# Three small moves in a four-layer decoder trunk: where the first weights land, which PSUM banks two tiles use, and when a broadcast product is issued

## The chip, the cores and the metric

The kernel runs on one core of one Trainium2 chip. A core has five engines with in-order instruction queues: TensorE (PE in the rows, its weight loads PEld), VectorE (DVE), ScalarE (ACT), GpSimd (POOL) and SyncE (SP), which here issues almost all transfers. The metric is the device time of one launch in microseconds; smaller is better.

## The reference, cut to what matters

The trunk has two layers on 256 tokens of width 2048. Layer 0 mixes tokens with a gated short convolution beside a state-space scan (S5), layer 1 with window attention. Both then attend to 256 memory tokens and run a gated MLP. What the change touches is all at the start:

```python
mem_n = rms_norm(mem, norm_mem)
hn = rms_norm(h, norm_mix[0])
z = hn @ w_in                      # gate B | gate C | conv input | S5 input u
ys = s5_branch(u, ...)             # a linear recurrence over the 256 tokens
k, v = jnp.split(mem_n @ w_kv[l], 2, axis=-1)   # for both layers l
```

Everything is in float32.

## The kernel before, in words

**Products in two parts.** Every matrix is split into a rounded part `hi` and a remainder `lo`. `wload` fetches 1 MB of weights into one of three `raw` buffers (SP, line 87), casts 1024 columns at a time to `hi` on ACT (line 95), and forms `lo = raw - hi` on DVE (line 96); there are four `hi` and four `lo` buffers, which is two weight tiles. A product tile of `gemm` is 16 matmuls with `hi` (line 110, 512 columns wide: the activations' own hi and lo side by side) and 16 with `lo` (line 115). The result sits in one of four large-pool PSUM banks (`pp`, tag `ps`) until ACT copies one half out (line 206) and DVE adds the other (line 210). Four more banks (`pm`, taken by `bank()`) serve all small products.

**Order of the start.** `first_tiles` runs through the 16 blocks k of the input and of the first 512 columns of u in steps of 1, 1, 2, 2, 2, 4, 4: load x (line 294), load the weights (line 87), split x with its gain (ACT line 72, DVE line 73), square it (ACT 223, POOL 221), and multiply into four banks at once (lines 311 and 314). Then four more u tiles, n = 4 to 7, go through `gemm` (weights `win(28)` to `win(31)`); the statistics product (line 235) and the broadcast product of the input's norm stand among them. Before, all weights of this stretch rotate through the three `raw` buffers.

**The memory's keys and values.** `mem_kv(0)` then runs 16 key tiles and 4 column groups of 4 value steps (matmuls of lines 371, 372 and 376), and `mem_kv(1)` the same for layer 1. After each tile a callback pulls pieces of the S5 work (`s5`, a generator) worth about 2 us: B products (line 440, which take all four small banks and are copied out by ACT, line 442), the scan itself (ACT line 541 and DVE lines 545 to 548, each step needing the other engine's last), and the outputs (lines 564 to 577). Key tiles collect in a single buffer `kst` of four tiles; when it is full ACT's queue issues its write to DRAM (line 361) and the next tile's DVE addition waits until that has landed.

**The memory's norm.** In layer 0's keys, `mem_norm` squares the memory tokens on ACT after tiles 5 and 6, computes the reciprocal root as a column after tile 8 (`rsqrt_col`, lines 243 to 252), and after tile 10 calls `stat_bc("mem")`: two DVE instructions write a diagonal matrix into a shared temporary (line 261), two matmuls with a matrix of ones spread it to all partitions (line 263), and ACT copies the result out (line 268). Its user, the cross-attention, comes hundreds of microseconds later.

**Who orders what.** Python order is program order; a scheduling layer assigns buffers and waits and may move an instruction ahead of others that its model holds up. Each engine then executes its own list strictly in order.

Of the kernel before, what the change touches and what calls it, by code (L numbers as in the profile page):

```python
# [13 lines left out]
F32 = mybir.dt.float32  # L14
# [3 lines left out]
ALU = mybir.AluOpType  # L18
# [4 lines left out]
P = 128  # L23
T = 256
D = 2048
KT = 16
# [10 lines left out]
class Trunk:  # L37
# [42 lines left out]
        nc.vector.tensor_tensor(o[:, T:], src, o[:, :T].bitcast(F32), op=ALU.subtract)  # L80
        return o

    def wload(self, src, kt, n):

        nc = self.nc
        raw = self.rawp.tile([P, kt * n], F32, name="raw", tag="raw")
        nc.sync.dma_start(raw.rearrange("p (k n) -> p k n", n=n), src)
        kc = 1024 // n
        parts = []
        for c in range(0, kt, kc):  # L90
            m = min(kc, kt - c)
            hi = self.hip.tile([P, m * n], F32R, name="hi", tag="hi")
            lo = self.lop.tile([P, m * n], F32R, name="lo", tag="lo")
            s = raw[:, c * n:(c + m) * n]
            nc.scalar.copy(hi, s)  # L95
            nc.vector.tensor_tensor(lo, s, hi.bitcast(F32), op=ALU.subtract)  # L96
            for j in range(m):
                parts.append((hi[:, j * n:(j + 1) * n], lo[:, j * n:(j + 1) * n]))
        return parts
# [21 lines left out]
            half()  # L121
        self.mm_lo(ps, w, ops, k0, k1, K)

    def gemm(self, src, n_tiles, ops, K, evac, late=0, pre=0, mid=None, mid2=None, after=None, one=False, half=None, end=None):

        n_tiles = list(n_tiles)
        held = []

        def start(i, k1):
            n = n_tiles[i]
            w = self.wload(src(n), K, P)
            ps = self.pp.tile([P, 512], F32, name="ps", tag="ps")
            self.mm(ps, w, ops, 0, k1, K, one(n) if callable(one) else one, half=None if half is None else lambda: half(n))
            return n, w, ps

        def finish(n, ps):
            evac(n, ps)
            if after is not None:  # L140
                after(n)
        for i in range(pre):
            held.append(start(i, K - late))
            if end is not None:
                end(n_tiles[i])
        if mid is not None:
            mid()
        for n, w, ps in held:
            self.mm(ps, w, ops, K - late, K, K, one(n) if callable(one) else one)
            if mid2 is None:  # L150
                finish(n, ps)
        i = pre
        if mid2 is not None:
            held.append(start(i, K))
            i += 1
            mid2()
            for n, w, ps in held:
                finish(n, ps)
        for i in range(i, len(n_tiles)):
            n, w, ps = start(i, K)  # L160
            finish(n, ps)
# [91 lines left out]
        self.rcol = y  # L253
        return y

    def stat_bc(self, tag="h", turned=False):

        nc = self.nc
        diag = self.t1()
        for b in range(2):  # L260
            nc.vector.tensor_scalar(diag[:, b * P:(b + 1) * P], self.ident, self.rcol[:, b:b + 1], None, op0=ALU.mult)
        pb = self.bank()
        nc.tensor.matmul(pb[:, :T], lhsT=self.ones, rhs=diag, start=True, stop=True)
        rbc = self.smp.tile([P, T], F32, name="rbc", tag="rbc_" + tag, bufs=1)
        if turned:
            nc.scalar.copy(rbc.rearrange("p (m b) -> p b m", b=2), pb[:, :T].rearrange("p (b m) -> p b m", b=2))
        else:
            nc.scalar.copy(rbc, pb[:, :T])
        self.rbc = rbc
        return rbc, pb  # L270
# [23 lines left out]
            nc.sync.dma_start(self.hc[:, k0:k1, :], I["xT"][:, k0:k1, :])  # L294
        return load_x

    def first_tiles(self, load_x, xs):

        ps = [self.pp.tile([P, 512], F32, name="ps", tag="ps") for _ in range(4)]
        self.stat_begin()  # L300
        lag = 4
        k = 0
        for step in (1, 1, 2, 2, 2, 4, 4):
            load_x(k, k + step)
            w = self.wload(self.I["ev_u0"][:, k:k + step, :], step, 512)
            for j in range(step):
                xs.append(self.split_gain(self.h[k + j], self.gain(G_MIX, k + j)))
                if k + j >= lag:
                    self.stat_add(self.h[k + j - lag])
                for n in range(4):  # L310
                    self.nc.tensor.matmul(ps[n], lhsT=w[j][0][:, n * P:(n + 1) * P], rhs=xs[k + j], start=k + j == 0, stop=False)
            for j in range(step):
                for n in range(4):
                    self.nc.tensor.matmul(ps[n][:, :T], lhsT=w[j][1][:, n * P:(n + 1) * P], rhs=xs[k + j][:, :T], start=False, stop=k + j == KT - 1)
            k += step
        for k in range(KT - lag, KT):
            self.stat_add(self.h[k])
        return ps
# [272 lines left out]
    def even_mixer(self):  # L591
        nc, tc = self.nc, self.tc
        load_x = self.setup()
        xs = []
        with tc.tile_pool(name="s5", bufs=1) as pool:
            win = lambda n: self.I["ev_w_in"][n]
# [9 lines left out]
                for n in ns:  # L606
                    nc.vector.tensor_tensor(u[n], u[n], rbc, op=ALU.mult)
            place = lambda shape: pool.tile(shape, F32, name="S", tag="S")
            ps = self.first_tiles(load_x, xs)
            for n in range(4):  # L610
                evac_u(n, ps[n])
            mem = place([P, KT, T])
# [22 lines left out]
                    scale_u((7,))  # L635
                    mem_step(8, 16)
            rbc = None
            self.gemm(lambda n: win(24 + n), range(4, 8), xs, KT, evac_u, after=after_u)
            r2 = self.smp.tile([P, T], F32, name="r2", tag="r2", bufs=1)
            nc.vector.tensor_tensor(r2, rbc, rbc, op=ALU.mult)  # L640

# [3 lines left out]
            def mem_norm(n):  # L645
                if n == 2:
                    mt["S"] = place([P, 2, D])
                    mt["ss"] = self.smp.tile([P, 2], F32, name="ss", tag="ss")
                    for b in range(2):
                        nc.sync.dma_start(mt["S"][:, b, :], self.I["mem_tok"][:, b, :])  # L650
                elif n in (5, 6):
                    b = n - 5
                    nc.scalar.activation(mt["S"][:, b, :], mt["S"][:, b, :], AF.Square, accum_out=mt["ss"][:, b:b + 1])
                elif n == 8:
                    self.mcol = self.rsqrt_col(mt["ss"], "mem")
                    self.load_consts()
                elif n == 10:
                    self.mrbc, _ = self.stat_bc("mem")

            bg = self.s5(pool, u, ys)  # L660
            st = {"left": 0.0}
# [1 line left out]
            def after(_, us=self.S5_US):  # L663
                st["left"] += us
                while st["left"] > 0:
                    c = next(bg, None)
                    if c is None:
                        st["left"] = -1e9
                        return
                    st["left"] -= c  # L670

            def after_k(n):
                mem_norm(n)
                after(n)
            self.kv = [self.mem_kv(l, pool, after if l else after_k, after) for l in range(2)]
            gc = {}

            def evac_gate(n, ps):
# [26 lines left out]
        evac, nxt = self.resid_evac(G_XA)  # L705
# [481 lines left out]
```

## Time and profile before

| | us |
|---|---|
| median of 3 runs | 2796.9 (2794.25 to 2797.08) |
| the profiled execution | 2794.98, of which the span is 2793.2 |
| PE busy in the span | 2766.6 (99%) |
| DVE busy | 1928.5 (69%) |
| ACT busy | 1556.8 (56%) |
| POOL busy | 212.8 (8%) |

The profile is one execution. Its timeline lists instructions by start, its wait view says for how long an engine sat idle before an instruction and whose end released it, and its window view gives the busy time of every engine in a stretch with the clock that TensorE was granted (1.00 is 2.4 GHz, 0.50 is 1.2 GHz). About 1.8 us lie outside the span. Shares over the whole span hide that the first 300 us, where the S5 work runs beside the products, look different from the rest.

### The profile page before, as it was taken

What the parts mean: (1) busy time and instruction counts of PE and PEld (TensorE: products, weight loads), DVE (VectorE), ACT (ScalarE), POOL (GpSimd) and SP (SyncE); (2) the same over time, 40 slices, a digit from 0 to 9 for tenths busy, and PEclk for the clock granted to TensorE, in tenths of its full rate; (3) what the DMA queues carried; (4) which work ended last, traced back from release to release, by engine and by line L of the source; (5) the groups of instructions that cost most, each with busy time, mean ns of one, the idle gap of its engine ahead of it and who ended that gap; (6) DMA issues with size and microseconds to landing.
All of it is one profiled execution on the core that took longest, in us unless ns stands there. A gap on an engine that the chain in (4) does not pass through costs nothing.

```text
span 2793.2 us, 39738 instructions
## 1 busy us (share of the span) xinstructions
PE 2766.6 (99%) x14980; PEld 2373.2 (85%) x14980; DVE 1928.5 (69%) x3115; ACT 1556.8 (56%) x2432; POOL 212.8 (8%) x237
## 2 busy tenths in 40 slices
PE   9999999999999999999999999999999999999998
PEld 8787878888988888888888888889888888888887
DVE  8978788867666666566566878776666665666665
ACT  7676766655554554454554566555555545545544
POOL 1000000001000010000010300000101000100113
PEclk9999999999999999999999999999999999999999
DMA  8665665555545766666666644464556766767654
GB/s 308 201 217 173 218 218 198 206 182 207 190 161 187 245 234 219 220 224 224 237 221 217 195 170 155 162 212 172 176 196 233 238 217 210 247 211 234 219 195 136
DMA packets 195378, 578.42 MB, mean 207 GB/s; under 512 B 95761, under 2 KB 122737, under 8 KB 144241
## 3 DMA queue, kind: packets, MB, share of 16 engines
q1 hardware_dynamic: 107776, 545.64, 56.9%
q10 hardware_dynamic: 87408, 30.24, 4.2%
q8 instruction: 117, 1.92, 0.3%
q14 instruction: 77, 0.62, 0.1%
HBM read 544.32 MB, written 31.51 MB: 206 GB/s over the span
## 4 chain that ended last, share of the span: by engine, by line
PE 94%; DVE 3%; ACT 2%; issue 1%; DMA 0%; SPq 0%; DVEq 0%; ACTq 0%
PE ps L110 35%; PE ps L179 21%; PE ps L115 18%; PE ps L183 10%; PE ps L371 2%; PE ps L372 2%; PE ps L376 2%; DVE lo L96 1%; PE m L934 1%; ACT stmp L541 1%; PE m L840 1%; ACT hi L95 1%; PE m L826 0%; PE m L794 0%; DVE S L546 0%
## 5 line engine op out<-in xcount | busy, mean ns | idle before, releaser
L96 DVE TENSOR_TENSOR lo<-raw,hi 128x1024 fp32r<-128x1024 f32 (+1 forms) x1001 | 1155.6, 1176 | 579.0 <-issue 221.4
L95 ACT CAST hi<-raw 128x1024 fp32r<-128x1024 f32 (+1 forms) x1001 | 994.4, 1008 | 897.9 <-PE ps L110 443.0
L110 PE MATMUL ps<-op,hi 128*128 128x512 f32 x4440 | 1078.2, 393 | 3.4 <-ACT hi L95 2.8
L110 PEld LDWEIGHTS ps<-op,hi 128*128 128x128 f32 x4440 | 813.6, 189 | 167.1 <-ACT hi L95 5.1
L179 PE MATMUL ps<-hi,op 128*128 128x512 f32 x2560 | 607.0, 389 | 0.0
L115 PEld LDWEIGHTS ps<-op,lo 128*128 128x128 f32 x4448 | 575.4, 191 | 25.4 <-DVE lo L96 1.4
L115 PE MATMUL ps<-op,lo 128*128 128x256 f32 x4448 | 588.4, 283 | 0.6 <-DVE lo L96 0.6
L179 PEld LDWEIGHTS ps<-hi,op 128*128 128x128 f32 x2560 | 480.0, 188 | 99.3
L183 PE MATMUL ps<-lo,op 128*128 128x512 f32 x1280 | 316.1, 389 | 0.0
L183 PEld LDWEIGHTS ps<-lo,op 128*128 128x128 f32 x1280 | 240.3, 188 | 49.9
L221 POOL TENSOR_TENSOR acc<-acc,t 128x256 f32<-128x256 f32 x98 | 92.5, 944 | 1147.7 <-ACT t L223 1145.5
L1012 POOL TENSOR_TENSOR zf<-zf,y 128x256 f32<-128x256 f32 x80 | 75.1, 969 | 1095.6 <-DMA zf<-zd 1056.1
L73 DVE SCALAR_TENSOR_TENSOR op<-h,gains,op 128x256 fp32r<-128x256 f32 x96 | 73.2, 771 | 86.4 <-ACT op L72 86.2
L541 ACT ACTIVATE stmp<-S,s_pw 128x256 f32<-128x256 f32 (+3 forms) x256 | 116.7, 521 | 27.1 <-DVE S L548 21.8
L371 PE MATMUL ps<-hi,op 128*128 128x512 f32 x256 | 101.0, 394 | 0.3 <-ACT hi L95 0.2
L372 PE MATMUL ps<-hi,op 128*128 128x512 f32 x256 | 99.8, 390 | 0.0
L206 ACT COPY t<-ps 128x256 f32<-128x256 f32 x130 | 47.4, 367 | 53.4 <-PE ps L115 50.4
L80 DVE TENSOR_TENSOR op<-zf,op 128x256 fp32r<-128x256 f32 x80 | 49.3, 628 | 32.5 <-ACT op L79 32.5
L546 DVE TENSOR_TENSOR S<-S,stmp 128x512 f32<-128x512 f32 (+11 forms) x92 | 60.8, 665 | 13.1 <-ACT stmp L541 12.9
L376 PE MATMUL ps<-lo,op 128*128 128x512 f32 x256 | 63.6, 390 | 0.7 <-DVE lo L96 0.7
L79 ACT CAST op<-zf 128x256 fp32r<-128x256 f32 x80 | 32.2, 406 | 51.8 <-POOL zf L1012 51.8
L371 PEld LDWEIGHTS ps<-hi,op 128*128 128x128 f32 x256 | 48.0, 188 | 12.8 <-ACT hi L95 1.6
(228 smaller groups left out, 1706.8 us busy)
## 6 DMA issues: line engine op xcount, KB each, us to landing
raw<-in_ff_gate_t SPq DMA_DIRECT2D x80, 1024.0 KB, 5.7
raw<-in_ff_up_t SPq DMA_DIRECT2D x80, 1024.0 KB, 5.9
raw<-in_ff_down SPq DMA_DIRECT2D x96, 768.0 KB, 4.9
raw<-in_xa_k SPq DMA_DIRECT2D x32, 1024.0 KB, 5.1
raw<-in_xa_v SPq DMA_DIRECT2D x32, 1024.0 KB, 5.1
raw<-in_xa_q SPq DMA_DIRECT2D x32, 1024.0 KB, 5.0
raw<-in_xa_o SPq DMA_DIRECT2D x32, 1024.0 KB, 4.9
raw<-in_ev_w_in SPq DMA_DIRECT2D x28, 1024.0 KB, 5.0
```

The lines of the kernel that those rows point to most:

```text
L95: nc.scalar.copy(hi, s)
L96: nc.vector.tensor_tensor(lo, s, hi.bitcast(F32), op=ALU.subtract)
L110: nc.tensor.matmul(ps, lhsT=hi, rhs=o, start=k == 0, stop=False)
L115: self.nc.tensor.matmul(ps[:, :T], lhsT=w[k][1], rhs=ops[k][:, :T], start=False, stop=k == K - 1)
L179: nc.tensor.matmul(ps[b], lhsT=xs[k][:, i * T + b * P:i * T + (b + 1) * P], rhs=w[j][0], start=k == 0 and i == 0, stop=False)
L183: nc.tensor.matmul(ps[b], lhsT=xs[k][:, b * P:(b + 1) * P], rhs=w[j][1], start=False, stop=k == KT - 1)
L221: nc.gpsimd.tensor_tensor(self.acc, self.acc, self.sq, op=ALU.add)
L371: nc.tensor.matmul(ps[b], lhsT=o[:, b * P:(b + 1) * P], rhs=w[j][0], start=k == 0, stop=False)
L372: nc.tensor.matmul(ps[b], lhsT=o[:, T + b * P:T + (b + 1) * P], rhs=w[j][0], start=False, stop=False)
L376: nc.tensor.matmul(ps[b], lhsT=self.memop[k][:, b * P:(b + 1) * P], rhs=w[j][1], start=False, stop=k == KT - 1)
L541: nc.scalar.activation(tmp[:, x, :, p - p0, :], at(0, both, p), AF.Copy, scale=pw[:, x, k, 8 * b + p:8 * b + p + 1])
L1012: nc.gpsimd.tensor_tensor(u[:, i, :], u[:, i, :], ys[i], op=ALU.mult)
```

## The change

1. `first_tiles` gets a tile `room` of the scan's pool (16 KB per partition, empty until the memory is loaded into the same place). The weights of blocks 0 to 7 land there; only blocks 8 to 15 use `raw` buffers.
2. In the second group of u tiles, n = 4 and n = 5 take their PSUM bank from the small pool instead of the large one.
3. The diagonal matrix of the memory norm is formed right after tile 8 in a tile of its own, into which the broadcast result is later copied as well; the two matmuls and the copy move from after key tile 10 of layer 0 to after key tile 4 of layer 1.

```diff
-    def wload(self, src, kt, n):
+    def wload(self, src, kt, n, raw=None):
         nc = self.nc
-        raw = self.rawp.tile([P, kt * n], F32, name="raw", tag="raw")
+        if raw is None:
+            raw = self.rawp.tile([P, kt * n], F32, name="raw", tag="raw")
         nc.sync.dma_start(raw.rearrange("p (k n) -> p k n", n=n), src)
...
-            ps = self.pp.tile([P, 512], F32, name="ps", tag="ps")
+            ps = self.pp.tile([P, 512], F32, name="ps", tag="ps") if place is None else place(n)
...
-    def stat_bc(self, tag="h", turned=False):
-        nc = self.nc
-        diag = self.t1()
+    def stat_diag(self, diag):
         for b in range(2):
-            nc.vector.tensor_scalar(diag[:, b * P:(b + 1) * P], self.ident, self.rcol[:, b:b + 1], None, op0=ALU.mult)
+            self.nc.vector.tensor_scalar(diag[:, b * P:(b + 1) * P], self.ident, self.rcol[:, b:b + 1], None, op0=ALU.mult)
+        return diag
+
+    def stat_bc(self, tag="h", turned=False, diag=None):
+        nc = self.nc
+        if diag is None:
+            diag = self.stat_diag(self.t1())
         pb = self.bank()
         nc.tensor.matmul(pb[:, :T], lhsT=self.ones, rhs=diag, start=True, stop=True)
-        rbc = self.smp.tile([P, T], F32, name="rbc", tag="rbc_" + tag, bufs=1)
+        rbc = diag if tag == "mem" else self.smp.tile([P, T], F32, name="rbc", tag="rbc_" + tag, bufs=1)
...
-            w = self.wload(self.I["ev_u0"][:, k:k + step, :], step, 512)
+            w = self.wload(self.I["ev_u0"][:, k:k + step, :], step, 512, room[:, 512 * k:512 * (k + step)] if k < 8 else None)
...
-            ps = self.first_tiles(load_x, xs)
+            ps = self.first_tiles(load_x, xs, place([P, 8 * 512]))
...
-            self.gemm(lambda n: win(24 + n), range(4, 8), xs, KT, evac_u, after=after_u)
+            self.gemm(lambda n: win(24 + n), range(4, 8), xs, KT, evac_u, after=after_u,
+                      place=lambda n: self.bank() if n < 6 else self.pp.tile([P, 512], F32, name="ps", tag="ps"))
...
                     self.mcol = self.rsqrt_col(mt["ss"], "mem")
+                    self.mdiag = self.stat_diag(self.smp.tile([P, T], F32, name="mdiag", tag="rbc_mem", bufs=1))
                     self.load_consts()
-                elif n == 10:
-                    self.mrbc, _ = self.stat_bc("mem")
...
+            def after_k1(n):
+                if n == 4:
+                    self.mrbc, _ = self.stat_bc("mem", diag=self.mdiag)
+                after(n)
...
-            self.kv = [self.mem_kv(l, pool, after if l else after_k, after) for l in range(2)]
+            self.kv = [self.mem_kv(l, pool, after_k1 if l else after_k, after) for l in range(2)]
```

## Rows read from the trace of the kernel before

**Rows 1.** Page, span and busy time: us, share, instructions.
```profile
span 2793.2 us, 39738 instructions
PE   2766.6 (99%) x14980; PEld 2373.2 (85%) x14980; DVE 1928.5 (69%) x3115; ACT 1556.8 (56%) x2432; POOL 212.8 (8%) x237
```

**Rows 2.** Waits of PE, whole span: us in total, times, longest.
```profile
PE m L263 <- DVE t L261: 8.7, 2, 6.0
PE ps L311 <- ACT hi L95: 2.8, 2, 2.2
...
PE ps L110 <- DVE u L210: 0.6, 1, 0.6
```

**Rows 3.** Timeline of PE around its longest wait: start, us, instructions [idle before].
```profile
119.44 1.78 PE L110 MATMUL ps<-op,hi 128*128 128x512 f32 x7
127.26 1.22 PE L263 MATMUL m<-t,ones 128*128 128x256 f32 x2 [6.05 <-DVE t L261]
127.92 3.77 PE L110 MATMUL ps<-op,hi 128*128 128x512 f32 x9
131.53 2.07 PE L115 MATMUL ps<-op,lo 128*128 128x256 f32 x16
```

**Rows 4.** Windows: busy us of PE, PEld, DVE, ACT, POOL; clock, DMA share, GB/s.
```profile
12.00:32.00 20.00, 20.00 (x110) 17.59 (x109) 20.00 (x22) 15.93 (x32) 10.58 (x12) 0.93 0.98 377
...
121.20:127.26 6.06, 0.02 (x1) 0.00 (x0) 5.99 (x12) 0.00 (x0) 0.00 (x0) 0.73 0.50 173
127.26:129.00 1.74, 1.74 (x4) 1.46 (x5) 1.71 (x4) 0.38 (x2) 0.00 (x0) 0.50 0.00 0
...
131.00:133.00 2.00, 2.00 (x16) 1.87 (x16) 1.36 (x8) 1.05 (x1) 0.00 (x0) 1.00 0.74 311
```

**Rows 5.** Timeline of DVE behind the wait.
```profile
126.75 0.46 DVE L261 TENSOR_SCALAR t<-ident,rcol 128x128 f32<-128x128 f32 x2
...
132.74 2.36 DVE L96 TENSOR_TENSOR lo<-raw,hi 128x1024 fp32r<-128x1024 f32 x2 [0.54 <-PE ps L115]
...
142.19 0.42 DVE L210 TENSOR_TENSOR kst<-ps,t 128x256 f32<-128x256 f32 x1 [0.42 <-ACT hi L95]
```

**Rows 6.** Timeline of ACT after it.
```profile
151.37 1.35 ACT L541 ACTIVATE stmp<-S,s_pw 128x126 f32<-128x126 f32 x3 [3.70 <-DVE S L548]
...
164.06 2.00 ACT L95 CAST hi<-raw 128x1024 fp32r<-128x1024 f32 x2 [2.60 <-DVE kst L210]
...
173.90 0.96 ACT L541 ACTIVATE stmp<-S,s_pw 128x254 f32<-128x254 f32 x2 [0.90 <-DVE S L548]
...
176.95 1.08 ACT L95 CAST hi<-raw 128x1024 fp32r<-128x1024 f32 x1
```

**Rows 7.** Timeline of PE at the second column group of layer 0's values.
```profile
178.68 0.39 PE L371 MATMUL ps<-hi,op 128*128 128x512 f32 x1
```

**Rows 8.** Timeline of the start: ACT, PE, DVE and SP.
```profile
8.35 0.91 ACT L72 ACTIVATE op<-h,gains 128x256 fp32r<-128x256 f32 x2 [1.39 <-DMA h<-in_xT]
...
10.86 3.39 PE L311 MATMUL ps<-op,hi 128*128 128x512 f32 x8 [2.18 <-ACT hi L95]
...
16.89 1.21 DVE L96 TENSOR_TENSOR lo<-raw,hi 128x1024 fp32r<-128x1024 f32 x1
...
5.46 0.33 SPq L87 DMA_DIRECT2D raw<-in_ev_u  x1
```

**Rows 9.** DMA issues at 2.59 and 12.72 us: KB, us to landing.
```profile
h<-in_xT SPq DMA_DIRECT2D x1, 256.0 KB, 5.7
...
h<-in_xT SPq DMA_DIRECT2D x1, 512.0 KB, 8.1
```

**Rows 10.** Timeline: a broadcast product unhindered, and one group of B products with its copies.
```profile
45.80 0.60 PE L263 MATMUL m<-t,ones 128*128 128x256 f32 x2
...
166.71 0.98 PE L440 MATMUL m<-us,BT 32*128 32x256 f32 x24
...
174.75 2.02 ACT L442 COPY S<-m 128x512 f32<-128x512 f32 x4
```

More of the change, by code (lines that the diff above doesn't have):

```diff
@@ L122, in mm, with gemm @@
         self.mm_lo(ps, w, ops, k0, k1, K)
-    def gemm(self, src, n_tiles, ops, K, evac, late=0, pre=0, mid=None, mid2=None, after=None, one=False, half=None, end=None):
+    def gemm(self, src, n_tiles, ops, K, evac, late=0, pre=0, mid=None, mid2=None, after=None, one=False, half=None, end=None, place=None):
         n_tiles = list(n_tiles)
@@ L254, in rsqrt_col @@
         return y
-    def stat_bc(self, tag="h", turned=False):
+    def stat_diag(self, diag):
+        for b in range(2):
+            self.nc.vector.tensor_scalar(diag[:, b * P:(b + 1) * P], self.ident, self.rcol[:, b:b + 1], None, op0=ALU.mult)
+        return diag
+    def stat_bc(self, tag="h", turned=False, diag=None):
         nc = self.nc
-        diag = self.t1()
-        for b in range(2):
-            nc.vector.tensor_scalar(diag[:, b * P:(b + 1) * P], self.ident, self.rcol[:, b:b + 1], None, op0=ALU.mult)
+        if diag is None:
+            diag = self.stat_diag(self.t1())
         pb = self.bank()
         nc.tensor.matmul(pb[:, :T], lhsT=self.ones, rhs=diag, start=True, stop=True)
-        rbc = self.smp.tile([P, T], F32, name="rbc", tag="rbc_" + tag, bufs=1)
+        rbc = diag if tag == "mem" else self.smp.tile([P, T], F32, name="rbc", tag="rbc_" + tag, bufs=1)
         if turned:
@@ L295, in setup, with first_tiles @@
         return load_x
-    def first_tiles(self, load_x, xs):
+    def first_tiles(self, load_x, xs, room):
         ps = [self.pp.tile([P, 512], F32, name="ps", tag="ps") for _ in range(4)]
```

## The prediction

> **What bounds the kernel now.** I read the page first: PE is busy for 2766.6 of 2793.2 us [rows 1], so only about 26.6 us of the span can be won from waits at all. Next the waits of PE, to see where those lie [rows 2]: 8.7 us in two waits for the diagonal of a norm (line 263), the longest of 6.0; 2.8 us in the first tiles for a cast; 0.6 us for a PSUM bank. Each of the three edits has its wait there. So the question is not whether the waits exist but whether PE, freed of them, runs into something else. For that I read the timeline around the long wait, the windows for the clock, and then DVE's and ACT's queues behind it, looking for gaps: a stretch in which an engine has none, or none that PE ends, will not shorten because PE comes earlier.
>
> **The long wait, and what it is worth at most.** PE had done seven of a tile's sixteen `hi` matmuls at 121.2 us and then stood 6.05 us before line 263 [rows 3]. In that stretch DVE worked 5.99 of 6.06 us [rows 4]: the diagonal (line 261) is not slow, 0.46 us [rows 5], it stands late in a full queue. The clock fell too. The granted share is 0.50 from 127.26 and 1.00 again from 131.00 [rows 4], after six idle microseconds; half of those 3.7 us is lost, 1.9 us. One sees it in the matmuls: nine took 3.77 us, seven before the wait 1.78 us [rows 3]. Ceiling of edit 3: 6.05 + 1.9 = 8.0 us.
>
> The diagonal is now formed right after its column, which the timeline has near 70 us, and the product stands behind key tile 4 of layer 1, some 200 us after that, so it cannot wait for it. The ceiling is therefore really removed at this place. What is late next?
>
> **What PE meets instead.** DVE was six microseconds behind PE when the wait began; the wait let it catch up. Without it the lag stays, and PE can draw on two tiles of buffers only. I follow the queues to the place where PE had the least in hand, the second column group of layer 0's values: its first cast ran from 176.95 to 178.03 [rows 6] and PE used it at 178.68 [rows 7], 0.65 us later. Eight microseconds earlier PE would be there at 170.7 and need a cast that was not done until 178.03. How far does that cast move? It stands in ACT's queue behind scan work, and each gap of ACT on the way, 3.70 us before 151.37, 2.60 before 164.06 and 0.90 before 173.90, is ended by DVE, by lines 548 or 210 [rows 6]. DVE in turn runs from 126.75 to 151.3 with two gaps only [rows 5]. The one of 0.54 us at 132.74 is ended by PE, which frees a `lo` buffer, and vanishes when PE is early. The one of 0.42 us at 142.19 stands before the first addition into a new `kst`; the view names ACT, but ACT's cast there was long over, so I put it down to the write of the old `kst`, which moves with the queue. The diagonal's slot (0.37 us, from 126.75 to the next start at 127.12) goes, but the same two instructions now stand near 70 us in front of the same chain, so I count nothing for them.
>
> So the scan's DVE and ACT work comes 0.5 us earlier, not 8. PE gains that and its 0.65 us in hand: 0.54 + 0.65 = 1.2 us. The other 6.8 us come back as several smaller waits of PE for `lo` and `hi` between 145 and 178 us. Bounds: from nothing (the chain does not move and the 0.65 is used up by the diagonal's earlier place) to all 8.0.
>
> A sentence of the Trainium skill speaks against this sum: its page "Perfetto Trace Analysis", section "Optimization Strategy", advises finding the gaps of the engine one optimises for, seeing what it waits for, and making that dependency start sooner; read alone it credits the gap in full, 8.0 us. Here the engine that is full during the gap is another one, so the row on DVE (5.99 of 6.06 us) bears on how much of the credit is kept [rows 4].
>
> **The moved product.** Two matmuls and a copy that stood at half clock beside the stall now stand in layer 1's keys. Unhindered the pair shows 0.60 us [rows 10]; the next matmul starts before its tail ends, so I take 0.3 us as my estimate, with 0 and 0.6 as ends. PE is the bound from there on, so it counts: +0.3. The copy joins ACT's queue, one instruction of 256 columns, hidden by ACT's waits for PE and transfers; uncovered it would be about that size again.
>
> **Weights in the room.** Only loads that used to wait for a buffer start earlier. The first such is that of blocks 4 and 5, issued at 5.46 us [rows 8]; those of blocks 0 to 3 are issued before and do not change. PE's wait of 2.18 us before 10.86 belongs to blocks 2 and 3, and ACT was held there until 8.35 by x itself [rows 8]. From 12 to 32 us PE and DVE are both busy for 20.00 of 20.00 us [rows 4], so weights that come sooner for blocks 4 to 7 find nobody free. I take 0. The lower end is the whole 2.8 us of these waits [rows 2]. The upper end: all loads now queue at once behind each other, and x for blocks 2 and 3 could share the transfer engines with them. It took 5.7 us from issue; the slowest x load, issued into a full queue, 8.1 us [rows 9]; so +2.4 us. I take 0 because nothing ahead of it in the queue has changed. SP gains too: the x loads behind the weights are no longer held. The memory's load now waits for the room, whose last reader, the remainder of blocks 6 and 7, is done at 16.89 + 1.21 = 18.1 us [rows 8]; it went out at about that time before, so nothing behind it in SP's queue is held longer.
>
> **Two tiles in small banks.** The 0.6 us before line 110 [rows 2] go: n = 4 no longer waits for the first evacuation. The four small banks hold n = 4, n = 5, the statistics and the broadcast, so none is short. But DVE's queue, full there, sets when the next diagonal is ready, 13 us later, and PE would wait for that. I take 0; without that cover it is -0.6.
>
> **Sum**, on the profiled execution: 2794.98 - 1.2 + 0.3 + 0 + 0 = 2794.1 us. That execution lies 1.9 us under the median of 2796.9; the four times known average 2795.8, and with 0.9 off that gives 2795, which I predict. A difference of 0.2%, 5.6 us, is about what a measurement of this kernel can tell from none; this is inside.
>
> **Rivals.** *Handed through in full* (faster): the order of the scan's pieces in DVE's and ACT's lists is made anew, or the buffers carry PE until the value steps, where it has more in hand. Then 8.0 + 0.6 us are kept: 2795.8 - 8.6 = 2787. For it: the lag arises in one stretch only, and after 180 us ACT waits for PE often. Against it: three gaps of ACT in a row that DVE ends. *A bank wait* (slower): the product takes a small bank, and all four go to each group of B products. The worst such row: products at 166.71, first copy out at 174.75, 8.0 us later [rows 10]. Stood the moved product behind such a group, PE would wait up to 8.0 us and lose another 1.9 to the clock: 2795.8 + 9.9 - 0.9 = 2805. It decides from a wait of 4.6 us (4.6 + 1.9 - 0.9 = 5.6). Against it: the nearest group comes after key tile 6, so the product has a tile and a half of room. *A late start*: x for blocks 2 and 3 comes 2.4 us later: 2797.3, inside the bound. *The wait only moves* (the change doesn't do what it says): the product would have to find its diagonal missing 200 us after it was made; I give that nothing of its own.
>
> **From this to the numbers.** Forecast 0.54, with its own range of 2792.5 to 2797; in full 0.30; bank wait 0.11; late start 0.05. Faster by over 0.2%: the full case and a little of the forecast's lower edge, 0.31. Slower: 0.11. Same: 0.58. The range reaches down to the full case and up past the late start, 2787 to 2798, and leaves out the bank wait and the far side of the full case.
>
> **What would show it.** Right: no wait at line 263 in the key tiles; between 145 and 180 us several waits of PE for lines 95 and 96, together 5 to 7 us; the first weights' loads issued in one row from 1 to 7 us with PE's start at 10.9 us unchanged; the first matmul of the second value group about 1 us earlier. Wrong: that matmul 6 us or more earlier with PE unbroken from 119 us (the full case); a wait at line 263 in layer 1 for a copy of line 442 (the bank); PE's third start later than 12 us (the loads).

## The result, and the profile after

The change made the kernel slower: 2800.89 us, the median of 18 runs (2797.89 to 2804.53), against 2796.57 of the kernel before beside it (2794.13 to 2798.09); the ratio is 1.0016 with a 95% interval of 1.0009 to 1.0023. The forecast was 2795.0, and its range ended at 2798. The rise of 0.16% is smaller than the 0.2% that the prediction took for the least that can be told from none; the interval is tighter than that, and 1 lies outside it.

The page of the kernel after: PE has 2.5 us more busy time than before [rows 1] in a span that is 6.8 us longer.

```profile
span 2800.0 us, 39734 instructions
PE 2769.1 (99%) x14980; PEld 2372.9 (85%) x14980; DVE 1930.5 (69%) x3115; ACT 1555.5 (56%) x2432; POOL 212.5 (8%) x237
```

The waits of PE over the whole span. Line 268 is line 263 of before, 317 is 311, 111 and 116 are 110 and 115, 377 and 382 are 371 and 376. The wait of 6.0 us for the memory's diagonal is gone, as is that for a bank [rows 2]; the 2.7 us left at line 268 are another norm's, at the very end of both kernels. What has grown is the wait for casts, above all for `lo` at line 116.

```profile
PE ps L116 <- DVE lo L97: 7.5, 8, 2.1
PE ps L111 <- ACT hi L96: 3.5, 5, 1.3
PE ps L317 <- ACT hi L96: 3.0, 3, 1.6
PE m L268 <- DVE t L259: 2.9, 2, 2.7
PE ps L377 <- ACT hi L96: 2.8, 4, 1.3
...
PE ps L382 <- DVE lo L97: 1.0, 1, 1.0
```

In the kernel before, the first of these was

```profile
PE ps L115 <- DVE lo L96: 0.6, 1, 0.6
```

The timeline of PE from where the stall stood before [rows 3] to the second column group of layer 0's values; only instructions with 0.4 us or more of idle time before them are copied here. The last row answers to [rows 7]: that matmul ran at 178.68 before and runs at 184.69 now.

```profile
125.42 2.35 PE L116 MATMUL ps<-op,lo 128*128 128x256 f32 x16 [0.47 <-DVE lo L97]
...
133.13 1.21 PE L116 MATMUL ps<-op,lo 128*128 128x256 f32 x8 [1.71 <-DVE lo L97]
...
149.47 1.22 PE L116 MATMUL ps<-op,lo 128*128 128x256 f32 x8 [2.09 <-DVE lo L97]
...
155.49 1.22 PE L116 MATMUL ps<-op,lo 128*128 128x256 f32 x8 [1.15 <-DVE lo L97]
...
165.27 0.50 PE L377 MATMUL ps<-hi,op 128*128 128x512 f32 x1 [1.01 <-ACT hi L96]
...
184.69 0.50 PE L377 MATMUL ps<-hi,op 128*128 128x512 f32 x1 [1.26 <-ACT hi L96]
```

To see where the time goes I took the same matmul of the large products in two traces and subtracted its start in the kernel before. This lag, in us, negative where the kernel is ahead, stands below for all kernels of this study; the head of a column is the time of the matmul in the kernel before. Each row is one execution. Differences of about a microsecond are not read: `room_only` moves by 1.2 between 560 and 2000 us, where nothing was edited. Where a kernel has moved the scan's own products in PE's list (the pause and the budgets below), its lag leaves out products that are still to come.

```
run                    50    117    130    142    150    166    181    400    560   2000
after                -1.2    1.7   -6.5   -2.0    0.4    4.6    6.2    6.7    6.7    6.8
banks_only           -1.1   -0.2    4.4    5.6    5.6    5.6    5.7    5.8    5.9    6.0
room_only             1.5    1.5    1.8    1.7    1.7    1.7    1.7    2.1    2.1    3.3
product_only          0.5    0.5   -7.8   -8.0   -5.6   -1.4    0.1    0.5    0.5    0.6
room_and_product      2.0    2.0   -6.3   -6.5   -3.9    0.4    1.9    2.4    2.5    3.9
after_early_load     -1.3   -1.3   -9.6   -9.8   -7.2   -3.0   -1.5   -1.2   -1.2    0.0
before_late_load      0.2    0.2    0.8    2.6    2.6    2.6    3.2    0.1    1.3    3.3
after_pause          -1.1   -1.1   -9.3   -7.0   -5.2   -2.4    0.6   -2.0   -0.8    0.2
early_load_pause     -0.4   -0.4   -8.6   -7.2   -3.5    0.8    0.3   -2.4   -1.2   -1.1
early_load_u17       -1.1   -0.6   -8.9   -5.7   -2.1    2.1    2.7   -0.7    3.6    3.8
early_load_u15       -2.1   -2.1  -10.3  -10.6   -9.6   -5.8   -5.0  -10.6   -2.9    2.1
after_scan_light     -2.0    1.0   -7.2   -5.4   -0.8    1.2    1.2    2.0    2.0    3.1
early_load_spread    -1.5   -1.5   -9.7   -9.9   -9.4   -5.6   -4.8   -4.7   -4.2   -3.2
early_pause_spread   -0.9   -0.9   -9.1   -9.3   -6.4   -2.3   -2.8   -2.7   -2.3   -2.3
early_load_spread2   -0.6   -0.6   -8.8   -9.0   -7.3   -3.7   -2.9   -2.2   -0.3   -2.0
params_on_pool       17.0   17.6    9.4    9.2    9.8   14.0   15.6   15.7   15.6   16.5
```

The first row reads: the stall's 8.2 us are won at 130 us (from +1.7 to -6.5), and 12.7 are lost between there and 181 (from -6.5 to +6.2). That is 4.5 more than the stall was worth, and another 2.9 were lost ahead of it, between 50 and 117 us. After 181 us next to nothing happens.

What differs ahead of that stretch is not on PE, which is busy for 45.00 us of the 45 from 54 to 99 us in both kernels, but on DVE. Windows, first of before, then of after (busy us of PE, PEld, DVE, ACT, POOL; clock, DMA share, GB/s):

```profile
54.00:99.00 45.00, 45.00 (x298) 39.58 (x297) 41.64 (x166) 31.91 (x51) 0.00 (x0) 1.00 0.77 268
```

```profile
54.00:99.00 45.00, 45.00 (x295) 39.42 (x294) 36.30 (x151) 30.11 (x49) 0.00 (x0) 1.00 0.66 227
```

DVE stands idle for 3.4 us there before and for 8.7 after, 5.3 more. Why, SP's timeline shows: `s5p`, the scan's parameters, 48 KB, whose place nobody edited. In the kernel before it is issued at 45.26 us:

```profile
45.26 0.42 SPq L447 DMA_DIRECT2D s5p<-in_s5p  x1
```

In the kernel after it stands five loads later in SP's list, behind both loads of `mem_tok` and three more key loads, which wait for free `raw` buffers (place 25 instead of 23, where a run of like loads counts as one place, here and in what was expected of the runs):

```profile
48.42 0.80 SPq L657 DMA_DIRECT2D S<-in_mem_tok  x2
53.74 3.62 SPq L88 DMA_DIRECT2D raw<-in_xa_k  x2
57.41 0.43 SPq L453 DMA_DIRECT2D s5p<-in_s5p  x1
```

DVE's list follows. The first instruction on the parameters, the first step of the exponential, starts at 55.00 us before and at 68.37 after, and the scan's first addition at 96.25 and at 102.52. In DVE's timeline after, the gaps lie where the exponential used to be, and before a write to `kst` (4.2 us, where the kernel before waits 1.6):

```profile
59.67 2.37 DVE L97 TENSOR_TENSOR lo<-raw,hi 128x1024 fp32r<-128x1024 f32 x2 [2.03 <-issue]
...
62.99 0.17 DVE L244 TENSOR_SCALAR v<-ss 128x2 f32<-128x2 f32 x1 [0.61 <-ACT S L660]
...
68.37 0.17 DVE L398 TENSOR_SCALAR s5p<-s5p 128x32 f32<-128x32 f32 x1
...
93.42 0.42 DVE L211 TENSOR_TENSOR kst<-ps,t 128x256 f32<-128x256 f32 x1 [4.23 <-DMA kv<-kst]
...
102.52 1.28 DVE L552 TENSOR_TENSOR S<-S,stmp 128x512 f32<-128x512 f32 x2
```

So theory A was: one of the edits made the planner lay the lists anew, the parameters' load came late, and the late scan holds PE. Its rivals: the product, the room or the banks cost time where they stand.

### The profile page after: what moved, and what is told of

It is laid out like the page before. It is cut to its first block, busy times and chain, and to the rows that moved or that the text cites. A ratio compares the mean times of both kernels' runs of the same rounds, so it can differ in the third digit from the quotient of the medians.

```text
span 2800.0 us, 39734 instructions
## 1 busy us (share of the span) xinstructions
PE 2769.1 (99%) x14980; PEld 2372.9 (85%) x14980; DVE 1930.5 (69%) x3115; ACT 1555.5 (56%) x2432; POOL 212.5 (8%) x237
## 4 chain that ended last, share of the span: by engine, by line
PE 90%; DVE 5%; ACT 2%; issue 1%; DMA 1%; SPq 0%; DVEq 0%; ACTq 0%
PE ps L111 33%; PE ps L180 21%; PE ps L116 17%; PE ps L184 10%; DVE lo L97 2%; PE ps L377 1%; PE ps L382 1%; PE ps L378 1%; ACT stmp L547 1%; PE m L946 1%; PE m L852 1%; ACT hi L96 1%; DMA kv<-kst 1%; DVE S L552 1%; DVE stmp L551 1%
## 5 line engine op out<-in xcount | busy, mean ns | idle before, releaser
L97 DVE TENSOR_TENSOR lo<-raw,hi 128x1024 fp32r<-128x1024 f32 x996 | 1152.1, 1178 | 579.9 <-issue 229.8
L96 ACT CAST hi<-raw 128x1024 fp32r<-128x1024 f32 x996 | 990.0, 1008 | 900.7 <-PE ps L111 430.8
```

## The experiments

**One part at a time.** Each kernel is the kernel before with some of the three edits, as the change has them; the other hunks are left out. Here and below, every kernel was timed beside the kernel before, whose median lay between 2796.1 and 2796.6 each time.

```diff
 banks_only:       + place=lambda n: self.bank() if n < 6 else self.pp.tile(...)
 room_only:        + self.first_tiles(load_x, xs, place([P, 8 * 512]))
 product_only:     + self.mdiag = self.stat_diag(...)   + after_k1
 room_and_product: the last two together
```

> The kernel before with n = 4 and n = 5 in small banks and nothing else. Theory A (the list): the bank edit alone re-sorts SP's list as in the kernel after, the small load of the scan's parameters goes from place 23 to place 25 and is issued near 57 us instead of 45, the first addition into the scan's state comes near 102 us instead of 96, and since the memory norm's stall is still there the kernel is slower than before by 3 to 8 us: 2800 to 2805. Rival B (the moved product or the room costs the time, not the banks): the wait of 0.64 for a bank goes and nothing else, 2796.

> The kernel before with the diagonal formed behind its column and the broadcast product in layer 1's keys, nothing else. Theory A: parameters' load at place 23, no stall at line 263 in the keys, several smaller waits between 130 and 180 us; my forecast's step says 1.2 us kept less 0.3 for the product, 2796; kept in full 2789. Rival B (the product costs the time): 2800 or more.

> The change without the banks. Theory A (the list): the parameters' load stays at place 23, the scan starts near 96 us as before, and the stall of 6.05 us is gone: between my forecast of 1.2 us kept and 8 us kept, 2789 to 2795. Rival B (the product or the room costs the time): as the kernel after, 2800 to 2801. Rival C (whatever is won before 180 us is paid back there): 2796 to 2797.

> The kernel before with the first weights in the scan's room and nothing else. The load of the parameters stays at place 23. My forecast's step (nobody is free to use it): 2796 to 2797. The late start that I gave 0.05: 2798 to 2799. Theory A allows either, but not 2800 or more.

| kernel | us | ratio to before | 95% interval |
|---|---|---|---|
| banks_only | 2800.78 | 1.0016 | 1.0007 to 1.0025 |
| product_only | 2795.72 | 0.9997 | 0.9988 to 1.0006 |
| room_and_product | 2796.96 | 0.9999 | 0.9990 to 1.0008 |
| room_only | 2797.28 | 1.0002 | 0.9993 to 1.0011 |

The banks alone cost all that the change costs, and the other two cost nothing that can be told. Nor do they win anything: `room_and_product` missed the 2789 to 2795 of theory A and came out as its rival C said, with all that is won before 180 us paid back there. `banks_only` puts `s5p` where the kernel after does (57.53 us) and idles DVE in the same stretch; its stall is still there and longer, 10.6 us instead of 6.0, since the diagonal stands in DVE's queue behind work that is now late (DVE is busy for 10.60 of the 10.70 us from 121.0 to 131.7):

```profile
PE m L263 <- DVE t L261: 10.6, 1, 10.6
```

`product_only` is the clean picture of my forecast: 8.0 us ahead at 142 us, level at 181. Its matmul at the second column group runs at 178.61, and [rows 7] had it at 178.68. Of the 8.1 us that it gives back, the waits in these rows make up 4.7; the clock was also at 0.50 behind the first of them (the window from 146 to 148 us), where sixteen `hi` matmuls took 5.42 us:

```profile
143.53 1.21 PE L115 MATMUL ps<-op,lo 128*128 128x256 f32 x8 [2.14 <-DVE lo L96]
144.58 5.42 PE L110 MATMUL ps<-op,hi 128*128 128x512 f32 x16
...
154.27 0.50 PE L375 MATMUL ps<-hi,op 128*128 128x512 f32 x1 [0.37 <-ACT hi L95]
...
159.21 0.50 PE L375 MATMUL ps<-hi,op 128*128 128x512 f32 x1 [1.02 <-ACT hi L95]
...
178.61 0.50 PE L375 MATMUL ps<-hi,op 128*128 128x512 f32 x1 [1.21 <-ACT hi L95]
```

**Only the load.** The kernel after, with the load taken out of the scan's code and written just before it; in SP's list it comes to place 20 instead of 25.

```diff
+            self.par = pool.tile([P, 3, 32], F32, name="s5p")
+            nc.sync.dma_start(self.par, self.I["s5p"])
             bg = self.s5(pool, u, ys)
...
-        par = pool.tile([P, 3, 32], F32, name="s5p")
-        nc.sync.dma_start(par, I["s5p"])
+        par = self.par
```

> The kernel after, whole, with one thing changed: the parameters of the scan are loaded right before the first piece of the scan is written down, not inside it, so that the load stands at place 20 of SP's list, ahead of all key loads. Theory A (the list): the exponentials start near 55 us, the first addition near 96 us, and the lag of 6 us that the kernel after has from 181 us on is gone: 2788 to 2795. Rival B (banks, room or product cost the time themselves): 2800 to 2801, as the kernel after.

2796.25 us, ratio 0.9999 (0.9990 to 1.0008): the loss is gone, by a place in a list. The exponential starts at 57.59 us, the first addition at 94.87, and DVE idles 2.4 us in the window in which it idled 8.7:

```profile
54.00:99.00 45.00, 45.00 (x293) 39.41 (x293) 42.58 (x169) 32.20 (x55) 0.00 (x0) 1.00 0.76 262
```

The figure is 1.3 us above what theory A gave (2788 to 2795): ahead by 9.8 us at 142 us, the kernel still hands 8.3 of them back by 181, as `product_only` does. Set against this kernel's row in the table of lags, the kernel after loses 3.0 us by 117 us and another 4.7 between 130 and 142, and nothing behind that.

**The load late without any of the edits.** The kernel before, with one added line.

```diff
         yield from inputs(0)
+        yield 8.0
         par = pool.tile([P, 3, 32], F32, name="s5p")
```

> The kernel before, stall and all, with one number added: a pause of 8.0 in the scan's pieces between the first inputs and the load of the parameters, so that the load falls to place 36 of SP's list and the exponentials stand behind further casts. None of the three edits is in it. Theory A (a late load makes the scan late, and the scan's list on DVE paces PE up to 181 us): as slow as the kernel with the banks alone or slower, 2801 to 2807, with a longer wait at line 263. Rival B (the place of the load only goes along with the loss, the small banks make it): 2796 to 2797.

2796.74 us, ratio 1.0001 (0.9992 to 1.0010). Theory A in this form failed: the load is later than in the kernel after (place 36), the first addition comes at 106.49, DVE idles 13.7 us from 54 to 99, and nothing is lost but 3 us that are made good by 400. The time is the one that rival B gave, but rival B, that the small banks make the loss, doesn't fit `after_early_load`, which has the small banks and no loss. So a late load and an idle DVE need not cost anything. But the line does a second thing: `after` spends a budget per tile on the scan's pieces, so a pause of 8.0 also writes every later piece behind later tiles. That gave theory D: what holds PE is the scan work that stands in DVE's list ahead of the casts that PE wants next; a load that comes late under an unchanged layout puts the same work, late, ahead of the same casts. The pause in the kernel after tests it:

> The kernel after with the pause of 8.0 in the scan's pieces that the kernel before had in the last run, nothing else: the load of the parameters falls to place 35, later than in the kernel after. Theory A in its first form (a late load makes the kernel slow): 2801 or more. Theory D (what holds PE is scan work that stands in DVE's list ahead of the casts of the tiles that PE wants next; a late load hurts only because the list was laid out for an early one, and the pause writes the scan's pieces behind later tiles): PE keeps most of the stall, 2789 to 2794.

2795.15 us, ratio 0.9995 (0.9986 to 1.0004): 5.7 us less than the kernel after, with the load still later (issued at 76.71) and DVE idle for 13.6 us of this window.

```profile
54.00:99.00 45.00, 45.00 (x294) 39.45 (x294) 31.37 (x97) 27.30 (x41) 0.00 (x0) 1.00 0.68 233
```

Theory A's first form is refuted. D's direction held, but not its size: the number, 2789 to 2794, was missed by 1 us, and PE does not keep most of the stall, since it is 0.6 us behind the kernel before at 181 us.

The traces show D directly. For one and the same `lo` cast (line 96 of before) at three places, the table has by how many us DVE starts it later than in the kernel before, and how much work on the scan DVE has done ahead of it (parameters, its `BT`, `us` and `cc` tiles, steps; each instruction counted up to the start of the next). The heads are the start of the cast in the kernel before.

```
                    DVE later at            scan's work ahead at     PE's lag
run                 93.6   125.3   179.6     93.6   125.3   179.6    at 181
before               0.0     0.0     0.0     19.1    34.7    58.4       0.0
product_only         0.3     0.6     0.5     18.9    34.8    58.0       0.1
room_only            1.7     1.8     1.9     19.0    34.6    58.3       1.7
banks_only           4.4     4.4     6.1     19.2    35.1    58.8       5.7
after                6.2     6.6     6.6     19.0    35.4    58.8       6.2
after_early_load    -1.4    -0.8    -1.0     18.4    34.4    57.7      -1.5
before_late_load     3.1     0.8     3.6     10.4    24.5    53.7       3.2
after_pause          2.8     0.3     1.0     10.4    24.5    53.7       0.6
early_load_u17       3.9     4.2     0.4     18.4    34.4    56.9       2.7
early_load_u15      -0.8    -2.9    -5.8     17.6    27.0    54.7      -5.0
early_load_spread   -0.9    -2.7    -5.6     17.7    27.0    54.7      -4.8
```

In the first six kernels the work ahead of each cast is the same to about a microsecond; what DVE is late by at 93.6 us it is still late by at 179.6 (`banks_only` adds 1.7), and PE's lag at 181 us is DVE's to half a microsecond. The kernel after has lost its 6.2 us by 93.6, and 5.3 of them are the idle time from 54 to 99. This is also why `product_only` wins nothing: DVE's list comes no earlier. With the pause, some 9 to 10 us of the scan's work have moved behind the first two of these casts, and more idle time costs less. So the late load costs what it leaves DVE idle in front of a list that is otherwise unchanged.

**DVE or ACT.** D speaks of DVE, but the scan alternates between DVE and ACT. The kernel after, its late load kept, without one of the three additions in each step of the scan's first block:

```diff
-                    v.tensor_tensor(at(m, 1, pa), at(m, 1, pa), tmp[:, 1, 0], op=ALU.add)
+                    if b:
+                        v.tensor_tensor(at(m, 1, pa), at(m, 1, pa), tmp[:, 1, 0], op=ALU.add)
```

> The kernel after with its late load, but the third addition of each step of the scan (the one into the imaginary part) left out in the scan's first block, so that part of the recurrence is missing. In the kernel after 22 of these stand on DVE between 100 and 185 us, 8.9 us by their durations, some 7 us of DVE's queue. Theory D (scan work on DVE ahead of the casts holds PE): the lag of 6.2 us at 181 us falls by 5 to 7, and the time to 2794 to 2796. Rival E (the chain through ACT's scaling holds it, or the loads): 2799 to 2801.

2796.7 us, ratio 1.0001 (0.9991 to 1.0010). The lag at 181 us falls from 6.2 to 1.2, the lower end of what D said, and the time by 4.2 us, 0.7 short of it. Of some 7 us taken off DVE's queue PE gets 5. This is not the removal alone, since the planner also moved some casts ahead of scan steps in DVE's list. Rival E's time, 2799 to 2801, did not come. The waits of the kernel after from 99 to 145 us, where it loses the 4.7 us, speak for DVE too; ACT waits for DVE, and DVE for nothing but one landing:

```profile
DVE kst L211 <- DMA kv<-kst: 2.0, 1, 2.0
```

```profile
ACT hi L96 <- DVE stmp L551: 13.0, 1, 13.0
ACT stmp L547 <- DVE S L554: 8.1, 1, 8.1
...
```

From 145 to 181 us ACT has a share: DVE waits 5.0 us for it there.

A second test of the same kind went wrong. It put the arithmetic on the parameters on GpSimd, with the load at place 15; a product-and-sum in one instruction becomes two.

```diff
-        nc.vector.tensor_scalar(n, x, 1.4426950408889634, MAGIC, op0=ALU.mult, op1=ALU.add)
+        nc.gpsimd.tensor_scalar(n, x, 1.4426950408889634, MAGIC, op0=ALU.mult, op1=ALU.add)
...
```

> The kernel after with the load of the scan's parameters at place 15 and the arithmetic on them (exponentials, sine's argument, powers; tiles of 128x32) on GpSimd instead of VectorE. In the trace of the kernel after with the early load these fill about 15 us of DVE between 57 and 91 us. Theory A (DVE's list paces PE up to 181 us): DVE reaches the first addition of the scan up to 15 us earlier, and PE keeps most of the 9.8 us that it is ahead at 142 us: 2786 to 2791, faster than both kernels. Rival B (ACT's scaling in the scan paces it, DVE's relief is no help): 2795 to 2797. Rival C (GpSimd is too slow for a chain of some 140 short operations and the scan starts later): 2800 or more.

2811.48 us, ratio 1.0051 (1.0039 to 1.0064), which is in rival C's range. It says nothing on D, since PE lost 17 us at 63 us to another cause: the chain on GpSimd was too slow, as rival C had it, but what it held up was ACT. ACT's timeline, then PE's:

```profile
60.34 0.23 ACT L475 ACTIVATE s_s<-s_th 128x32 f32<-128x32 f32 x1 [16.39 <-POOL s_th L474]
```

```profile
63.67 1.22 PE L268 MATMUL m<-t,ones 128*128 128x256 f32 x2 [16.66 <-DVE t L259]
```

The sine stood in ACT's list ahead of the copy of a `u` tile out of its bank, the chain on GpSimd was not ready, and behind ACT waited DVE, and behind DVE the mixer's own norm and PE. The Trainium skill, "PSUM — Partial Sum Buffer", "Engine vs sequencer instructions", states that the queues of ScalarE, VectorE and GpSimd are strictly first in, first out. The trace agrees: the copy waited out the 16.39 us behind the sine.

**Sparser, and where the time comes back.** If D holds, fewer scan pieces for each tile keep what the stall gave. With the early load: the pause, and smaller budgets for the key tiles.

```diff
-    S5_US, S5_V, S5_G = 2.0, 2.1, 1.8
+    S5_US, S5_V, S5_G = 1.7, 2.1, 1.8      (early_load_u17; 1.5 in early_load_u15)
```

> The kernel after with the early load (place 20) and the pause of 8.0: exponentials early, but the scan's steps written behind later tiles. Theory D: most of the 9.8 us that the early load alone is ahead at 142 us stays, 2787 to 2792. Theory A: not slower than the early load alone, 2796, and not faster, since the scan does not begin earlier.

> The kernel after with the early load, and the scan's budget for each key tile cut from 2.0 to 1.7, so that the same pieces are spread over more tiles. Theory D: fewer pieces ahead of each tile's casts; part of the 8.3 us that come back between 142 and 181 us stays won: 2789 to 2794. Theory A: 2796.

> As the run before with a budget of 1.5. Theory D: more of it stays, 2787 to 2792, unless the scan's end is now late for the gates. Theory A: 2796.

| kernel | us | ratio to before | 95% interval |
|---|---|---|---|
| early_load_pause | 2791.56 | 0.9983 | 0.9974 to 0.9992 |
| early_load_u17 | 2798.70 | 1.0008 | 0.9999 to 1.0017 |
| early_load_u15 | 2796.85 | 1.0001 | 0.9992 to 1.0010 |

The pause is inside D's range; 1.7 missed both ranges on the slow side, and 1.5 missed D's main range and took the exception that D had named. It shows both halves of D: it is still 10.6 us ahead at 400 us, 2.5 of them products of the scan that it has yet to run, and from 520 us on loses it all, because the scan ends late: its last addition starts at 568 us, and at 533 in `early_load_spread` below. Between 520 and 590 us it loses 10.9 us; the idle time in these rows is 5.0 of them, and the last row is a wait for the scan's own output:

```profile
531.03 3.92 PE L111 MATMUL ps<-op,hi 128*128 128x512 f32 x16 [0.94 <-ACT hi L96]
...
544.03 4.29 PE L111 MATMUL ps<-op,hi 128*128 128x512 f32 x16 [0.75 <-ACT hi L96]
...
551.77 3.96 PE L111 MATMUL ps<-op,hi 128*128 128x512 f32 x16 [1.54 <-ACT hi L96]
...
580.52 0.70 PE L579 MATMUL m<-yg,glu 128*128 128x256 f32 x2 [1.79 <-ACT yg L574]
```

1.7 went the wrong way: a lag of 2.7 at 181 us where 2.0 has -1.5, with DVE 3.9 us late at 93.6 us already and no less work ahead. A smaller budget moves whole pieces across tiles, not a little of each, and the lists are laid anew with it; which of the two made DVE late was not followed. So I put back later what the first tiles are spared.

```diff
+    S5_US, S5_V, S5_G = 1.5, 2.1, 2.0      (early_load_spread; 1.5, 2.2, 2.2 in spread2)
...
+                after(n, 2.3)              (layer 1's keys; 2.4 in spread2)
...
+    S5_US, S5_V, S5_G = 2.0, 2.1, 2.0      (early_pause_spread, with the pause; layer 1's keys 2.2)
```

> The kernel after with the early load and budgets of 1.5 for the key tiles of layer 0, 2.3 for those of layer 1, 2.1 for the values and 2.0 for the gates (2.0, 2.0, 2.1 and 1.8 before): the scan is sparse where PE was held and denser where the side engines have room. Theory D with room later: the 10 us that the budget of 1.5 kept up to 400 us stay, 2785 to 2790. Rival F (the total of the side work up to 560 us is the bound, wherever it is put): 2794 to 2797.

> As early_load_spread with 1.5, 2.4, 2.2 for the values and 2.2 for the gates. Theory D with room later: 2785 to 2790. Rival F: 2794 to 2797.

> The kernel after with the early load and the pause of 8.0, and budgets of 2.0 for layer 0's keys, 2.2 for layer 1's, 2.1 for the values and 2.0 for the gates. Theory D: as the early load with the pause or a little better, 2788 to 2792. Rival F: 2791 to 2795.

| kernel | us | ratio to before | 95% interval |
|---|---|---|---|
| early_load_spread | 2791.56 | 0.9981 | 0.9972 to 0.9990 |
| early_load_spread2 | 2791.77 | 0.9986 | 0.9977 to 0.9995 |
| early_pause_spread | 2792.15 | 0.9986 | 0.9977 to 0.9995 |

All three, and the pause with the early load, beat both kernels, by 4.0 to 4.7 us against before and some 9 against after; none reaches 2790. The first of them waits for casts 4.2 us between 99 and 190 us:

```profile
PE ps L382 <- DVE lo L97: 1.9, 2, 1.7
PE ps L377 <- ACT hi L96: 1.6, 1, 1.6
PE ps L116 <- DVE lo L97: 0.7, 1, 0.7
```

For the first two, neither "room later" (2785 to 2790) nor rival F (2794 to 2797) has it; the third is a hair above D's range and inside F's. In the first, of the 9.9 us ahead at 142 us, 4.8 are left at 181 and 3.2 at 2000.

## Why the prediction was wrong, step by step

- *The ceiling of 8.0 us for the stall.* Right. `product_only` goes from +0.5 to -7.8 there, 8.3 us.
- *Most of it comes back behind DVE.* Right, and more than I said: 7.9 of them are gone by 181 us in `product_only` (-7.8 to +0.1), where I had 6.8. The 1.2 us that PE was to keep were not kept: DVE's list came 0.3 to 0.6 us later, not 0.5 earlier, and the 0.65 in hand were worth nothing that the trace shows. The advice of the Trainium skill that I weighed, in "Perfetto Trace Analysis", "Optimization Strategy", to make what the engine waits for start sooner, puts no number on the gain; my reading of it alone, all 8.0 us, did not come true. In the trace of `product_only` 0.4 of the 8.3 us are left at 181 us.
- *The moved product, 0.3 us.* Not told apart from nothing; `product_only` as a whole is at 0.9997.
- *The room, 0.* Within the measurement. The start differs from run to run: the kernel after has the full clock from 12 to 32 us where [rows 4] has 0.93, but so has `before_late_load`, which has no room. The 1.2 us that the kernel after is ahead at 50 us are those of the banks: `banks_only` is 1.1 ahead without the room. With the room alone the wait for a bank is longer, 1.6 us instead of 0.6, and the lag at 50 us is 1.5.
- *The banks, 0, and -0.6 without cover.* **This step failed.** They cost 4.2 us. I costed the wait that goes away and looked at who is short of a bank; that loads might change places I weighed for the room alone, not for the banks. The wait did go, and 1.1 us of gain are there at 50 us. But the order of the lists is not the order of the code; it is made anew for each kernel, and the edit to two tiles moved a load of 48 KB, two hundred lines away, from 45 to 57 us. DVE stood idle for it and was 4.4 us late at 93.6 us, and PE came out 5.7 late at 181. My rivals had the lists made anew only in the direction in which that helps (*handed through in full*).
- *The range.* It reached up past the late start, 2797.3. The bank wait, at 2805, I left out. The measured 2800.9 lies between the two, and I had no case for a list laid anew that costs time.

What stays open: why the planner moves the load when two tiles change their bank was not tried; only that it does (place 23 without the banks, 25 with them, in every combination of the three edits that was run) and what it costs are shown. Of the 5.3 us that DVE idles more in the kernel after, 2.6 are the longer wait for the write of `kst`; it goes with the late load (1.4 us of wait with the load early), but why the write lands later was not followed. Nor was what takes the rest in the spread kernels.

## What to carry to other kernels

Where a program lays out the engines' lists, an edit is priced only when the new lists are known: compare them first, place by place, above all small loads in a queue of large ones that wait for buffers. A stall of the busiest engine is worth something only as far as the engine it waited for can run ahead too: count that engine's idle time, and the work that stands in its list ahead of what is wanted next. Put loads that gate a chain where they can be issued without waiting for anybody's buffer, or write the chain's later work behind later tiles, as the pause did; and lay background work sparse where the side engine is full and dense where it has room.

## What the runs showed of the hardware

Dependent instructions on DVE's small tiles (2 and 32 columns) start 0.19 to 0.23 us apart; where two independent chains alternate, 0.07 to 0.13. The same chain of the memory norm stood alone in the kernel after, and between the exponential's steps with the early load. Kernel after, then the early load:

```profile
63.99 0.16 DVE L253 SCALAR_TENSOR_TENSOR rcol<-rt,rcol 128x2 f32<-128x2 f32 x1
64.19 0.16 DVE L251 TENSOR_TENSOR rt<-rcol 128x2 f32<-128x2 f32 x1
```

```profile
64.05 0.15 DVE L251 TENSOR_TENSOR rt<-rcol 128x2 f32<-128x2 f32 x1
64.16 0.18 DVE L409 TENSOR_SCALAR ex_q<-ex_q 128x32 f32<-128x32 f32 x1
64.25 0.17 DVE L410 TENSOR_SCALAR ex_r<-ex_n 128x32 f32<-128x32 f32 x1
64.34 0.15 DVE L252 SCALAR_TENSOR_TENSOR rt<-rt,v 128x2 f32<-128x2 f32 x1
```

GpSimd's small instructions start 0.2 to 0.4 us apart while DVE stands still and 1.1 to 1.2 us apart while DVE runs the casts of line 97, one of which takes 1.2. POOL's timeline of `params_on_pool`, beside a row of casts on DVE from 27.64 to 32.3 us, and in DVE's wait that ends at 60.98:

```profile
29.12 1.06 POOL L393 TENSOR_SCALAR stw<-ex_n 128x32 f32<-128x32 f32 x1
30.26 1.02 POOL L394 TENSOR_TENSOR ex_r<-stw,s5p 128x32 f32<-128x32 f32 x1
...
49.85 0.22 POOL L409 TENSOR_SCALAR ex_q<-ex_r 128x32 f32<-128x32 f32 x1
50.15 0.25 POOL L411 TENSOR_TENSOR ex_q<-ex_q,ex_r 128x32 f32<-128x32 f32 x1
```

The Trainium skill, "GPSIMD Engine Reference", "1. Specifications", has GpSimd share its SBUF interfaces with VectorE, in contention where a DVE instruction has two inputs in SBUF. Line 97 has two, and the rows agree.
